# Two kinds of score matmuls in a bidirectional linear-attention block: in turn, or one kind after the other

## The chip, the cores and the metric

The kernel runs on one core of one Trainium2 chip. The metric is the device time of one execution in microseconds (us). The time before is the median of three executions; beside it stands one more execution, taken with the hardware profiler, from which all rows below come.

## What is computed

The program is two layers of an encoder trunk over 512 tokens of width 1024. A layer normalises its input, projects it, feeds three mixers (a state-space scan, a gated linear attention, a neighbourhood attention), mixes their outputs with gates and ends with a two-matrix MLP. The change touches the gated linear attention alone (GLA: 4 heads, key width 128, value width 256, chunks of 64 tokens, once forward and once backward). Cut to what matters, the reference computes for each head and direction:

```python
b = jnp.cumsum(g, axis=2)                       # log decay inside a chunk of 64
q_dec = q * jnp.exp(b)
att = jnp.einsum('bclhk,bcshk->bchls', q_dec, k * jnp.exp(-b))
att = jnp.where(tril, att, 0.0)                 # scores inside a chunk
o_intra = jnp.einsum('bchls,bcshv->bclhv', att, v)
states = jnp.einsum('bclhk,bclhv->bchkv', k * jnp.exp(b_last[:, :, None] - b), v)
...                                             # scan over the chunks
o_inter = jnp.einsum('bclhk,bchkv->bclhv', q_dec, s_prev)
```

## The kernel before, in words

All activations stay feature-major (128 features on the partitions, 512 tokens along the row). Most of the program is `feat` (L297) and `token` (L309): a weight of 128 x 1024 arrives by DMA, ScalarE rounds it to a high part (L285), VectorE subtracts to get the low part (L287), and TensorE multiplies in three products (L304 to L306, or L321 to L323) into a PSUM tile `pf` or `pt`. Three weights are under way at a time.

`gla_mix` (L649) is one head of the linear attention. Four pieces of 128 tokens (index `i`) hold two chunks of 64 each. For each direction `d` it builds on VectorE, ScalarE and GpSimd the decayed query `qd` (the tile `G_t`), two key tiles `ki` (`G_t` with 128 keys per piece, `G_kx` with 64) and the state keys `kw` (`G_w`). Then, at L694 to L702, it fills one PSUM tile `at` (a single buffer, `G_at`) per direction:

```python
T.matmul(at[:, i, b_], lhsT=ki[d][0][:, P * i: P * i + P], rhs=qs[0], start=True, stop=True)
T.matmul(at[a_, i, a_], lhsT=ki[d][1][:, i], rhs=qs[1], start=True, stop=True)
```

The first (L699) loads a weight of 128 columns and writes all 128 partitions; the second (L700) loads 64 columns and writes the 64 partitions `a_`. Both stream 64 query columns and contract over 128 rows. They are plain float32, and the hardware runs each as two passes, a weight load (LDWEIGHTS) and a matmul each: in the trace "x2" behind one of these lines is one such matmul. Two masked copies on VectorE (L701, L702) take `at` to the SBUF tiles `zt`, and GpSimd adds those to `G_A` (L704). After the scores, `kw` is transposed (L719) and copied (L721), the states are made (L731, L736, L738), and the output `po` is accumulated (L746, L748, L750). There are 2 layers x 4 heads x 2 directions = 16 of these blocks, each of four L699 and four L700.

The order of instructions on each engine is chosen at build time by a scheduler with a cost model: a block's matmuls are set between the `pf` or `pt` matmuls of the next projection, so that TensorE has other work while a head's VectorE work goes on. Each engine then runs its list strictly in that order.

Of the kernel before, what the change touches and what calls it, by code (L numbers as in the profile page):

```python
# [16 lines left out]
P = 128  # L17
# [182 lines left out]
def trunk(tc, a, out, layers=L, dbg=None):  # L200
    nc = tc.nc
    V, S, G, T = nc.vector, nc.scalar, nc.gpsimd, nc.tensor
    with ExitStack() as ctx:
# [178 lines left out]
        for l in range(layers):  # L382
# [263 lines left out]
            c4 = lambda ap, o: ap.rearrange("p (i o s) -> p i o s", i=4, o=2)[:, :, o]  # L646

            def gla_mix(h, q_, k_, v_, g_):
                qd, ki, kw, el, lg = [], [], [], [], []  # L649
# [44 lines left out]
                for d in range(2):  # L694
                    at = ph.p("at", (P, 4, P))
                    a_, b_ = slice(64 * d, 64 * d + 64), slice(64 - 64 * d, 128 - 64 * d)
                    for i in range(4):
                        qs = c4(qd[d], 1 - d)[:, i], c4(qd[d], d)[:, i]
                        T.matmul(at[:, i, b_], lhsT=ki[d][0][:, P * i: P * i + P], rhs=qs[0], start=True, stop=True)  # L699
                        T.matmul(at[a_, i, a_], lhsT=ki[d][1][:, i], rhs=qs[1], start=True, stop=True)  # L700
                    V.copy_predicated(zt[d][:, :, b_], trim[d][:, :, b_], at[:, :, b_])  # L701
                    V.copy_predicated(zt[d][a_, :, a_], trim[d][a_, :, a_], at[a_, :, a_])  # L702
                A = ph.t("A", (P, 4, P))
# [23 lines left out]
                for n in range(3):  # L727
                    pst_ = ph.p("at" if n == 2 else "x", (P, 2, 256))
                    for d in range(2):
                        i = n if d == 0 else 3 - n  # L730
                        T.matmul(pst_[:, d], lhsT=kt_[d][:, i], rhs=vv[i], start=True, stop=True)  # L731
                    for d in range(2):
                        i = n if d == 0 else 3 - n
# [56 lines left out]

            cur = gla_proj(0)
            y0 = gla_mix(0, *cur)
            for j in range(8):
                branch(0, j, nah, nal)
            gla_out(y0)
            cur = gla_proj(1)
            for h in range(1, 4):
                y = gla_mix(h, *cur)
                if h < 3:
                    cur = gla_proj(h + 1)  # L800
                    gla_out(y)
# [272 lines left out]
```

## Time and profile before

| | |
|---|---|
| median of 3 executions | 2468.46 us (2467.49 to 2468.6) |
| the profiled execution | 2469.9 us, span 2468.1 us |
| TensorE matmuls (PE) | busy 2452.2 us, 99% of the span, 12656 instructions |
| TensorE weight loads (PEld) | 2064.9 us, 84%, beside PE |
| VectorE (DVE) | 1425.8 us, 58% |
| ScalarE (ACT) | 1162.1 us, 47% |
| GpSimd (POOL) | 393.3 us, 16% |
| DMA engines, mean busy share | 31%, 101 GB/s |
| granted TensorE clock, mean | 0.998 of full speed |

PE's busy time counts a matmul from its start to a modelled end, so that it also covers time in which the array empties or waits for a weight. How long a piece of TensorE's work takes is therefore read from the distance between starts. On a timeline, a start is in us from the beginning of the span, and a group "x2" is two instructions in a row, its duration the time that they cover together.

### The profile page before, as it was taken

To read this page: it belongs to the slowest core of one execution; us is meant where nothing else is said; L and a number is where in the kernel's file an instruction comes from. 1 tells how busy PE (TensorE), PEld (TensorE's weight loads), DVE (VectorE), ACT (ScalarE), POOL (GpSimd) and SP (SyncE) were. 2 spreads that over 40 slices of the span, in tenths; PEclk is the share of its full clock that TensorE was granted. 3 is DMA by queue.
4 is the path that set the end of the run, shared out by engine and by line. 5 is a ranking of instruction groups with operands and counts; after the bars stand their busy time and mean duration, and the time that the engine had idled before them with its cause. 6 is when DMAs were issued, how large, how long until landed. Compare 5 with 4: busy or idle time off the path is not lost.

```text
span 2468.1 us, 32626 instructions
## 1 busy us (share of the span) xinstructions
PE 2452.2 (99%) x12656; PEld 2064.9 (84%) x12656; DVE 1425.8 (58%) x2148; ACT 1162.1 (47%) x2055; POOL 393.3 (16%) x333
## 2 busy tenths in 40 slices
PE   8999999999999999999999999999999999999999
PEld 7888889988788888888888888899878888888887
DVE  6776534587976554444447755345889665434443
ACT  4575435555855342332335654255568543422321
POOL 3132101112431110000122221011124312100000
PEclk9999999999999999999999999999999999999999
DMA  5221222223533322322332222222245333222232
GB/s 185 94 88 61 89 94 79 69 69 119 178 116 120 99 97 94 98 99 94 124 128 94 82 72 79 94 71 78 77 129 168 108 128 101 96 94 96 93 103 86
DMA packets 84603, 249.38 MB, mean 101 GB/s; under 512 B 9824, under 2 KB 15840, under 8 KB 84448
## 3 DMA queue, kind: packets, MB, share of 16 engines
q1 hardware_dynamic: 84016, 246.85, 30.5%
q8 instruction: 100, 1.64, 0.3%
q14 instruction: 55, 0.45, 0.1%
q10 hardware_dynamic: 432, 0.45, 0.1%
HBM read 242.80 MB, written 4.46 MB: 100 GB/s over the span
## 4 chain that ended last, share of the span: by engine, by line
PE 96%; DMA 2%; DVE 1%; ACT 1%; issue 0%; SPq 0%; DVEq 0%
PE pf L304 14%; PE pf L305 14%; PE pf L306 14%; PE F_pf L306 11%; PE F_pf L305 11%; PE F_pf L304 11%; PE pt L322 3%; PE pt L321 2%; PE pt L323 2%; PE N_po L569 2%; PE N_pt L562 1%; PE S_x L944 1%; PE G_at L699 1%; PE S_py L933 1%; PE G_at L700 1%; PE S_x L916 1%
## 5 line engine op out<-in xcount | busy, mean ns | idle before, releaser
L285 ACT ACTIVATE wh<-wr 128x1024 fp32r<-128x1024 f32 x378 | 400.2, 1059 | 938.7 <-PE F_pf L305 429.7
L287 DVE TENSOR_TENSOR wl<-wr,wh 128x1024 fp32r<-128x1024 f32 x378 | 485.7, 1285 | 188.4 <-ACT wh L285 186.6
L304 PE MATMUL pf<-xh,wh 128*128 128x512 f32 x1232 | 486.2, 395 | 7.6 <-DVE gl L592 3.7
L305 PE MATMUL pf<-xl,wh 128*128 128x512 f32 x1232 | 486.6, 395 | 0.7 <-DVE xl L349 0.7
L306 PE MATMUL pf<-xh,wl 128*128 128x512 f32 x1232 | 486.2, 395 | 0.0
L304 PEld LDWEIGHTS pf<-xh,wh 128*128 128x128 f32 x1232 | 232.2, 189 | 57.0 <-DVE gl L592 4.6
L306 PEld LDWEIGHTS pf<-xh,wl 128*128 128x128 f32 x1232 | 232.3, 189 | 49.5 <-issue 1.5
L305 PEld LDWEIGHTS pf<-xl,wh 128*128 128x128 f32 x1232 | 232.4, 189 | 48.9 <-issue 1.2
L304 PE MATMUL F_pf<-Ah,wh 128*128 128x512 f32 x640 | 248.4, 389 | 0.0
L306 PE MATMUL F_pf<-Ah,wl 128*128 128x512 f32 x640 | 247.8, 389 | 0.0
L305 PE MATMUL F_pf<-Al,wh 128*128 128x512 f32 x640 | 247.8, 389 | 0.0
L306 PE MATMUL F_pf<-xh,wl 128*128 128x512 f32 x512 | 200.1, 391 | 0.0
L305 PE MATMUL F_pf<-xl,wh 128*128 128x512 f32 x512 | 199.3, 389 | 0.0
L304 PE MATMUL F_pf<-xh,wh 128*128 128x512 f32 x512 | 199.3, 389 | 0.0
L1051 DVE TENSOR_TENSOR F_x<-F_x,F_pf 128x512 f32<-128x512 f32 x64 | 44.0, 688 | 205.6 <-PE F_pf L306 205.6
L322 PE MATMUL pt<-wl,xh 128*128 128x256 f32 x512 | 146.1, 286 | 0.0
L323 PE MATMUL pt<-wh,xl 128*128 128x256 f32 x512 | 145.9, 286 | 0.0
L321 PE MATMUL pt<-wh,xh 128*128 128x256 f32 x512 | 144.9, 284 | 0.0
L304 PEld LDWEIGHTS F_pf<-Ah,wh 128*128 128x128 f32 x640 | 120.2, 188 | 25.0
L305 PEld LDWEIGHTS F_pf<-Al,wh 128*128 128x128 f32 x640 | 120.1, 188 | 25.0
L306 PEld LDWEIGHTS F_pf<-Ah,wl 128*128 128x128 f32 x640 | 120.1, 188 | 24.8
L1044 DVE SCALAR_TENSOR_TENSOR F_v<-F_pf,rx 128x512 f32<-128x512 f32 x64 | 44.1, 691 | 159.5 <-PE F_pf L306 159.5
(313 smaller groups left out, 4257.1 us busy)
## 6 DMA issues: line engine op xcount, KB each, us to landing
wr<-pk SPq DMA_DIRECT2D x378, 512.0 KB, 3.3
N_bias<-bias SPq DMA_DIRECT2D x48, 256.0 KB, 2.9
S_E<-acd SPq DMA_DIRECT2D x32, 256.0 KB, 4.3
S_eB<-acd SPq DMA_DIRECT2D x32, 256.0 KB, 3.8
S_eb<-ead SPq DMA_DIRECT2D x64, 96.0 KB, 3.5
F_x<-xt SPq DMA_DIRECT2D x15, 256.0 KB, 5.2
xd<-F_x SPq DMA_DIRECT2D x8, 256.0 KB, 2.0
F_x<-xd SPq DMA_DIRECT2D x8, 256.0 KB, 4.8
```

The source lines that it names most:

```text
L285: S.activation(hi, raw, AF.Copy)
L287: V.tensor_tensor(lo, raw, f(hi), ALU.subtract)
L304: T.matmul(ps, lhsT=hi[:, c], rhs=rh[k], start=k == 0, stop=False)
L305: T.matmul(ps, lhsT=hi[:, c], rhs=rl[k], start=False, stop=False)
L306: T.matmul(ps, lhsT=lo[:, c], rhs=rh[k], start=False, stop=k == KT - 1)
L321: T.matmul(o, lhsT=rh[k][:, s], rhs=hi[:, c], start=k == 0, stop=False)
L322: T.matmul(o, lhsT=rh[k][:, s], rhs=lo[:, c], start=False, stop=False)
L323: T.matmul(o, lhsT=rl[k][:, s], rhs=hi[:, c], start=False, stop=k == KT - 1)
L562: T.transpose(pt[:, i, kb], s[:, i, P * kb: P * (kb + 1)], ident)
L569: T.matmul(po[r, P * cb: P * (cb + 1)], lhsT=vv[:, v0 + kb, r], rhs=ptS[:, i, kb], start=kb == 0, stop=kb == 1)
L1044: V.scalar_tensor_tensor(v_, ps, 0.0, rbc, ALU.max, ALU.mult)
L1051: V.tensor_tensor(xT[j], xT[j], ps, ALU.add)
```

## The change

Per direction, the loop over the four pieces is split in two: first the four matmuls with 128 keys, then the four with 64 keys. Operands, results and the number of instructions stay as they are.

```diff
                     at = ph.p("at", (P, 4, P))
                     a_, b_ = slice(64 * d, 64 * d + 64), slice(64 - 64 * d, 128 - 64 * d)
                     for i in range(4):
-                        qs = c4(qd[d], 1 - d)[:, i], c4(qd[d], d)[:, i]
-                        T.matmul(at[:, i, b_], lhsT=ki[d][0][:, P * i: P * i + P], rhs=qs[0], start=True, stop=True)
-                        T.matmul(at[a_, i, a_], lhsT=ki[d][1][:, i], rhs=qs[1], start=True, stop=True)
+                        T.matmul(at[:, i, b_], lhsT=ki[d][0][:, P * i: P * i + P], rhs=c4(qd[d], 1 - d)[:, i],
+                                 start=True, stop=True)
+                    for i in range(4):
+                        T.matmul(at[a_, i, a_], lhsT=ki[d][1][:, i], rhs=c4(qd[d], d)[:, i], start=True, stop=True)
                     V.copy_predicated(zt[d][:, :, b_], trim[d][:, :, b_], at[:, :, b_])
                     V.copy_predicated(zt[d][a_, :, a_], trim[d][a_, :, a_], at[a_, :, a_])
```

In the changed kernel these lines are L698 and L701, and every later line is one further down (L719 is L720 there, L731 is L732). On TensorE, the first block of the program (head 0, forward; `G_x` the transposed keys, `pf` the projection that goes on) ended before with these rows, the last two of its four turns:

```order
L699 MATMUL G_at_2817<-G_t_25_2770,G_t_26_2771 128x64
L700 MATMUL G_at_2817<-G_t_25_2770,G_kx_2798 64x64
L699 MATMUL G_at_2817<-G_t_25_2770,G_t_26_2771 128x64
L700 MATMUL G_at_2817<-G_t_25_2770,G_kx_2798 64x64
L719 MATMUL G_x_2845<-con,G_w_2793 128x128 x4
L305 MATMUL pf_2992<-xl_175,wh_2921 128x512
```

And the same place in the changed kernel, with the whole block and the projection matmul ahead of it:

```order
L304 MATMUL pf_2992<-xh_174,wh_2921 128x512
L698 MATMUL G_at_2817<-G_t_25_2770,G_t_26_2771 128x64 x4
L701 MATMUL G_at_2817<-G_t_25_2770,G_kx_2798 64x64 x4
L720 MATMUL G_x_2845<-con,G_w_2793 128x128 x4
L305 MATMUL pf_2992<-xl_175,wh_2921 128x512
```

The eight matmuls stand in two runs of four instead of eight runs of one, in this block and in the 15 others (96 rows fewer on TensorE, six a block); what stands before and after them here is the same.

Around the backward blocks of heads 1 and 2 the scheduler also moved a few neighbours by one or two projection matmuls. On TensorE, head 1, backward, where the states (`G_x`, `G_at` at L731, now L732) are made ("-" the kernel before, "+" the changed one):

```order
+L732 MATMUL G_at_3885<-G_gvg_3586,G_kwT_3858 128x256
+L732 MATMUL G_x_3871<-G_gvg_3586,G_kwT_3869 128x256
+L732 MATMUL G_x_3878<-G_gvg_3583,G_kwT_3858 128x256
+L732 MATMUL G_x_3878<-G_gvg_3586,G_kwT_3869 128x256
+L732 MATMUL G_at_3885<-G_gvg_3583,G_kwT_3869 128x256
 L323 MATMUL pt_4055<-wh_3935,xl_179 128x256
-L731 MATMUL G_at_3885<-G_gvg_3586,G_kwT_3858 128x256
-L731 MATMUL G_x_3871<-G_gvg_3586,G_kwT_3869 128x256
-L731 MATMUL G_x_3878<-G_gvg_3583,G_kwT_3858 128x256
-L731 MATMUL G_x_3878<-G_gvg_3586,G_kwT_3869 128x256
-L731 MATMUL G_at_3885<-G_gvg_3583,G_kwT_3869 128x256
```

The state matmuls stand ahead of one projection matmul that they stood behind; the other moves are of the same kind. VectorE's list has a few swaps in heads 1 and 2: L710 (L711 after), which overwrites the query `qd` that the block reads, now stands ahead of L682 in head 1 and ahead of L677 in head 2. The lists of ScalarE, GpSimd and the DMA queue are the same but for line numbers.

## Rows read from the trace of the kernel before

**Rows 1.** Page, part 1: busy time of the engines; part 4: chain by engine.

```profile
PE 2452.2 (99%) x12656; PEld 2064.9 (84%) x12656; DVE 1425.8 (58%) x2148; ACT 1162.1 (47%) x2055; POOL 393.3 (16%) x333
...
PE 96%; DMA 2%; DVE 1%; ACT 1%; issue 0%; SPq 0%; DVEq 0%
```

**Rows 2.** Windows: busy us per engine, then granted clock, DMA share, GB/s.

```profile
280.00:560.00 280.00, 280.00 (x1583) 244.66 (x1582) 155.73 (x255) 133.05 (x202) 29.66 (x22) 1.00 0.23 78
1506.00:1786.00 280.00, 280.00 (x1582) 244.74 (x1582) 156.12 (x255) 133.40 (x202) 29.66 (x22) 1.00 0.24 78
500.00:560.00 60.00, 60.00 (x282) 49.72 (x281) 51.85 (x84) 34.27 (x52) 8.07 (x5) 1.00 0.21 71
```

**Rows 3.** Tile G_at: line, engine, count, min/median/max ns, first and last start.

```profile
L699 PE MATMUL G_at<-G_t,G_t x128: 217/275/324, 284.0 to 1756.7; 128*128 128x64 f32 x128
L700 PE MATMUL G_at<-G_t,G_kx x128: 221/246/271, 284.3 to 1757.0; 128*64 128x64 f32 x128
```

**Rows 4.** Timeline of PE, first block: start, duration, line, shape, passes.

```profile
284.00 0.33 PE L699 MATMUL G_at<-G_t,G_t 128*128 128x64 f32 x2
284.26 0.33 PE L700 MATMUL G_at<-G_t,G_kx 128*64 128x64 f32 x2
284.52 0.43 PE L699 MATMUL G_at<-G_t,G_t 128*128 128x64 f32 x2
284.88 0.33 PE L700 MATMUL G_at<-G_t,G_kx 128*64 128x64 f32 x2
...
286.39 0.66 PE L719 MATMUL G_x<-con,G_w 128*128 128x128 f32 x4
```

**Rows 5.** Timeline of PEld (weight loads), same block; then one load each by tile.

```profile
284.52 0.30 PEld L699 LDWEIGHTS G_at<-G_t,G_t 128*128 128x128 f32 x2
284.88 0.19 PEld L700 LDWEIGHTS G_at<-G_t,G_kx 128*64 128x64 f32 x2
...
L699 PEld LDWEIGHTS G_at<-G_t,G_t x128: 185/188/192, 283.8 to 1756.7; 128*128 128x128 f32 x128
L700 PEld LDWEIGHTS G_at<-G_t,G_kx x128: 132/134/137, 284.3 to 1757.0; 128*64 128x64 f32 x128
```

**Rows 6.** Timeline, PE: runs of one shape elsewhere (2, 128 and 128 columns streamed).

```profile
75.04 0.95 PE L501 MATMUL N_v<-bsr,sq 128*128 128x2 f32 x8
...
607.92 1.50 PE L916 MATMUL S_x<-S_xw,S_bt 128*128 128x128 f32 x12
...
123.47 0.60 PE L569 MATMUL N_po<-N_pT,N_vb 128*64 128x128 f32 x4
```

**Rows 7.** Timeline, PEld: one short run; chain: a matmul of 256 columns, two passes.

```profile
567.49 0.32 PEld L813 LDWEIGHTS S_x<-con,gtmp 32*128 32x128 f32 x4 [0.35 <-issue]
...
306.20 0.43 PE G_po L748 x2
```

**Rows 8.** Timelines of DVE and PE: blocks and states, what they wait for or release.

```profile
289.85 0.43 DVE L702 COPY_PREDICATED zt<-con,G_at 64x256 f32<-64x256 int32 x1
291.90 0.33 PE L699 MATMUL G_at<-G_t,G_t 128*128 128x64 f32 x2
...
413.37 0.33 PE L700 MATMUL G_at<-G_t,G_kx 128*64 128x64 f32 x2
413.75 0.69 DVE L682 TENSOR_TENSOR G_t<-G_t,G_q 128x512 f32<-128x512 f32 x1
...
542.38 0.86 DVE L738 SCALAR_TENSOR_TENSOR G_st<-G_st,de,G_at 128x256 f32<-128x256 f32 x2
544.62 0.59 PE L748 MATMUL G_po<-G_st,G_t 128*128 128x256 f32 x2
```

**Rows 9.** Timeline of PE at a wait in the state-space part; windows behind it.

```profile
622.11 0.49 PE L304 MATMUL pf<-xh,wh 128*128 128x512 f32 x1 [2.08 <-DVE gl L592]
...
620.00:624.00 4.00, 1.92 (x8) 1.31 (x7) 3.96 (x11) 4.00 (x12) 0.00 (x0) 0.93 0.70 252
624.00:628.00 4.00, 4.00 (x28) 3.38 (x28) 3.96 (x8) 4.00 (x13) 1.07 (x1) 0.64 0.52 162
```

## The prediction

> **What bounds the kernel.** I read the page first. PE is busy 2452.2 us of a span of 2468.1 us, and the chain of work that ended last lies on PE for 96% of the span [rows 1]. So TensorE's own list sets the time, and a piece of it that gets shorter shortens the run, as long as nothing that it then reaches sooner is late. Second, the windows over the linear-attention stretch of either layer: PE is covered for 280.00 of 280.00 us in both, at a granted clock of 1.00 (the 2.4 GHz level), while VectorE is covered for 155.73 and ScalarE for 133.05 [rows 2]. In these stretches lie all 16 blocks of the change [rows 3], by their first and last start, so there is no wait in them that could swallow what a block saves.
>
> Third, the timeline of one block, for the time between starts. An L699 that follows an L700 begins at 284.52, the next L700 at 284.88: a turn of 0.36 us. An L700 begins at 284.26 and the next L699 at 284.52: a turn of 0.26 us [rows 4]. The whole block, from the first L699 at 284.00 to the first transpose at 286.39, takes 2.39 us. That is the first L699, whose first weight was loaded beside the projection matmul ahead of it (284.00 to 284.26, 0.26 us), three turns of 0.36 and four of 0.26, together 2.38 us.
>
> Fourth, what a turn is made of. Two weight loads of L699 cover 0.30 us and one is recorded with 0.188, so the second starts 0.11 us after the first; for L700 it is 0.19 less 0.134, or 0.06 us [rows 5]. Two loads would be 0.22 and 0.12 us. The turns are longer by 0.36 - 0.22 = 0.14 and by 0.26 - 0.12 = 0.14 us. The same 0.14 us stands behind either kind, each time where a weight of 128 columns and one of 64 follow each other: the next load does not start until the matmul before it has left the array. Where the shape stays the same, no such gap is to be seen. Eight passes of L501 (128 columns, two streamed) cover 0.95 us, twelve of L916 cover 1.50 us; with a record of 0.25 to 0.28 us for the last one, that is 0.10 and 0.11 us a pass [rows 3, 6]. Four passes of L569, which loads 64 columns and streams 128, cover 0.60 us, or 0.11 a pass. So runs of one shape go at the rate of their loads or of their matmuls, with no gap of 0.14 between them.
>
> **The change, part by part.**
>
> *The order inside a block.* Before, the shape changes at each of the eight turns' ends: eight switches. After, it changes twice, behind the last L699 and behind the last L700. Six switches go, per block 6 x 0.14 = 0.84 us. Written out: the L699 run takes 0.26 for the first and 3 x 0.22 for the rest, which is 0.92 us with the switch at its end; the L700 run takes 3 x 0.12 + 0.26 = 0.62 us; together 1.54 instead of 2.38 us. Over 16 blocks that is 16 x 0.84 = 13.4 us.
>
> *The unknown in it* is how fast a long run of 64-column loads with 64 streamed columns goes, since no row shows one longer than two passes. Bounds: the load's own distance inside a pair is 0.06 us, and a run of four passes at L813 covers 0.32 us with 0.13 to 0.14 for the last load, 0.06 a pass [rows 7]. The far end is L569 with 0.11 a pass [rows 6], but there twice as many columns stream. I take 0.06, since the streamed width is that of L700. At 0.11 an L700 turn in the run would be 0.22 and save only 0.04; a block would save 3 x 0.14 + 3 x 0.04 = 0.54 us, and the sum would be 8.6 us. At the other end the gap is 0.15 us where the roundings of 0.01 fall the other way, and the sum is 16 x 6 x 0.15 = 14.4 us.
>
> *What is reached sooner.* Each thing that PE reaches behind a block now comes up to 0.84 us earlier. The backward scores need `at` free again: L702 ends at 290.28 and the next block starts at 291.90, 1.62 us of room. The closest that I found is L748 behind L738, 543.24 to 544.62, 1.38 us, and L738 itself waits for PE's states, so it moves along [rows 8]. Both are larger than 0.84 us, so I cost them at nothing; the cover is TensorE's projection work, and if it were gone a wait would take back at most what a block saves.
>
> *The moved neighbours.* State matmuls that pass a projection matmul of 256 columns come some 0.1 us sooner, which the room above also covers. Their shape is the projection's, so no switch is added. The masked copy L701 may start sooner, because L699's results are complete earlier; no one waits for it, so nothing is gained. On VectorE, L710 may not run before the block has read `qd`, and it now stands ahead of L682 in head 1, in the slot at 413.75, with L682 and the next block's keys queued behind it. The last L700 began at 413.37 and covered 0.33 us [rows 8], so it was done at 413.70, and will be done 0.84 us sooner: no wait. DMA issues and the other engines' lists stand as before.
>
> *The sum.* 13.4 us off the profiled 2469.9 us gives 2456.5 us. That execution lies 1.4 us above the median of the others; the same 13.4 us off the median of 2468.46 us gives 2455.0 us, 0.54% less.
>
> **Rivals.**
>
> *Loads do not run ahead in a run.* If a load had to wait for the matmul ahead of it whenever both use the same rows, a pass would be load plus matmul. A matmul of 256 columns takes 0.43 / 2 = 0.215 us [rows 7], one of 64 then 0.05; passes become 0.16 and 0.11, turns 0.32 and 0.22, each 0.04 less than now. A block saves 3 x 0.04 + 3 x 0.04 = 0.24 us and the time is 2468.46 - 3.8 = 2464.6 us. Against it: L916 has a load of 0.11 and 128 streamed columns, also 0.11, and a pass takes 0.11, not 0.22 [rows 6]. In the Trainium skill, the page "TensorE: Matmul & The Clock Gate", part 3, section "The mechanism", says that a weight load overlaps with matmuls in flight only when their row groups differ. Both kinds here contract over all 128 rows, so by that rule the gain would be this small one. The trace of L916 disagrees with it: its loads and matmuls use the same 128 rows and overlap. Chance 0.05.
>
> *The gain is partly taken by waits.* The last two blocks of a layer lie in a stretch where VectorE is covered for 51.85 of 60 us [rows 2]. If VectorE could not move forward there, and the state-space part behind it then waited, up to 2 x 2 x 0.84 = 3.4 us would be lost, and with the 0.11 us pass the gain would fall to 5.2 us: 2463.3 us. Chance 0.05.
>
> *Slower: a new wait that drops the clock.* Where PE waited 2.08 us for VectorE at 622.11, the clock granted shortly after was 0.93 and 0.64 of full speed in two windows of 4 us [rows 9]: a part of the time at the 1.2 GHz level, worth 4 x 0.07 + 4 x 0.36 = 1.7 us. If every head's L748 came to wait as long, 8 x (2.1 + 1.7) = 30.4 us would be lost against 13.4 gained: 2485.5 us. It decides once L738 is late by more than its 1.38 us of room in all heads; nothing in the change delays it. Chance 0.02.
>
> *The change does not do what it says.* A scheduler could set the kinds in turn again; the rows of the order above show two runs of four, so this has no chance of its own.
>
> **How the numbers follow.** The forecast, a gain of 8.6 to 14.4 us, has a chance of 0.88. The clock's fall at 622 may or may not come in another run, which moves the time by 1.7 us either way. So the time lies between 2468.46 - 14.4 - 1.7 = 2452.4 and 2468.46 - 8.6 = 2459.8 us; I give 2452.0 to 2460.0. About 0.2% (4.9 us) is what a measurement of this kernel can tell from no change. The forecast and the partly taken gain lie beyond it (0.93), the rival with loads held back lies within (0.05), the new wait is slower (0.02).
>
> **What would show it.** In the changed profile, a block from its first L698 to the first L720 should take 1.5 to 1.6 us; eight passes of L698 should start 0.11 us apart and eight of L701 0.06; one gap of some 0.14 us should be left between the kinds and one at the end. PE should still cover the whole linear-attention stretch, now some 7 us shorter per layer. The forecast is wrong if blocks take over 1.9 us, or if they take 1.5 us and PE shows waits behind L732, L747 or L749 that were not there.

## The result, and the profile after

The changed kernel takes 2454.40 us (median of 6 executions, 2453.42 to 2455.18) against 2467.67 us of the kernel before (6 executions, 2465.82 to 2468.6). The ratio is 0.9946, with a 95% interval of 0.9934 to 0.9957: 13.3 us less. The forecast was 2455.0 us, from 13.4 us less.

The first lines of the page of the changed kernel, to be held against [rows 1]: PE is busy 13.3 us less, the other engines within 3 us of what they were.

```profile
span 2452.7 us, 32628 instructions
PE 2438.9 (99%) x12656; PEld 2057.8 (84%) x12656; DVE 1423.0 (58%) x2148; ACT 1161.7 (47%) x2055; POOL 394.8 (16%) x333
```

The timeline of PE over the first block (start, duration, line, shape, passes), which answers to [rows 4], and under it that of the weight loads, which answers to [rows 5]:

```profile
283.57 1.00 PE L698 MATMUL G_at<-G_t,G_t 128*128 128x64 f32 x8
284.50 0.68 PE L701 MATMUL G_at<-G_t,G_kx 128*64 128x64 f32 x8
285.11 0.66 PE L720 MATMUL G_x<-con,G_w 128*128 128x128 f32 x4
285.52 0.48 PE L305 MATMUL pf<-xl,wh 128*128 128x512 f32 x1
```

```profile
283.34 1.09 PEld L698 LDWEIGHTS G_at<-G_t,G_t 128*128 128x128 f32 x8
284.50 0.54 PEld L701 LDWEIGHTS G_at<-G_t,G_kx 128*64 128x64 f32 x8
```

From the first score matmul to the first transpose the block takes 285.11 - 283.57 = 1.54 us, where it took 2.39 us; the two runs take 0.93 and 0.61 us. All 16 blocks agree within 0.01 us. Eight loads of 64 columns cover 0.54 us, and with 0.138 us for the last [the tile's rows below] that is 0.058 us a load.

The tile's rows (count, then min/median/max ns, first and last start), against [rows 3] and [rows 5]:

```profile
L698 PE MATMUL G_at<-G_t,G_t x128: 217/275/275, 283.6 to 1739.9; 128*128 128x64 f32 x128
L701 PEld LDWEIGHTS G_at<-G_t,G_kx x128: 132/138/138, 284.5 to 1740.5; 128*64 128x64 f32 x128
```

The longest record of a 128-key matmul falls from 324 to 275 ns: it was the one that began behind a change of shape.

Windows over the linear-attention stretches, against [rows 2] (length of the window, busy us of PE, PEld, DVE, ACT, POOL, then clock, DMA share, GB/s):

```profile
280.00:552.00 272.00, 272.00 (x1578) 240.14 (x1577) 153.65 (x252) 132.49 (x201) 29.64 (x22) 1.00 0.24 79
1498.00:1770.00 272.00, 272.00 (x1579) 240.13 (x1578) 153.64 (x251) 131.61 (x200) 29.65 (x22) 1.00 0.24 79
```

PE is still covered from end to end; no wait took the place of the gaps. To see where the time went I cut the span at three marks in each layer: the first gate projection of the linear attention (`G_ga`), the first transpose of the state-space part (`S_x<-con,gtmp`) and the first matmul of the output projection (`F_pf`). Between the first two, both layers went from 298.56 to 291.74 us, 6.82 us less each, which is 8 blocks x 0.85 us. Between the last two, the state-space part and what follows it went from 280.35 to 277.91 us in the first layer and from 277.64 to 278.73 us in the second. The rest of a layer did not move (647.46 us from the first layer's output projection to the second layer's gate projection in both kernels).

The two profiled executions differ by 15.4 us of span, 2 us more than the medians. The piece above what the blocks gave, 1.8 us, lies in the state-space parts (1.4 us in sum) and at the start (0.4 us). That one of these parts shrank and the other grew is in part the clock: the fall that stood at 624 us before [rows 9] is gone, though the wait ahead of it is still there (2.1 us, at 613 us now), and another stands in the second layer, behind the same kind of wait (1.86 us, up to 1830.40). Windows of the changed kernel, the first over the wait at 613 us and what follows it:

```profile
612.00:628.00 16.00, 14.47 (x87) 11.71 (x89) 15.93 (x32) 13.84 (x41) 6.94 (x5) 1.00 0.61 202
1826.00:1830.00 4.00, 2.54 (x12) 1.75 (x11) 4.00 (x11) 3.29 (x9) 0.82 (x2) 1.00 0.72 222
1830.00:1834.00 4.00, 3.60 (x11) 2.46 (x13) 3.93 (x8) 4.00 (x12) 0.00 (x0) 0.58 0.37 95
```

### The profile page after: what moved, and what is told of

Read it like the earlier page. It is cut to its first block, busy times and chain, and to the rows that moved or that the text cites. A ratio compares the mean times of both kernels' runs of the same rounds, so it can differ in the third digit from the quotient of the medians.

```text
span 2452.7 us, 32628 instructions
## 1 busy us (share of the span) xinstructions
PE 2438.9 (99%) x12656; PEld 2057.8 (84%) x12656; DVE 1423.0 (58%) x2148; ACT 1161.7 (47%) x2055; POOL 394.8 (16%) x333
## 4 chain that ended last, share of the span: by engine, by line
PE 97%; DMA 1%; DVE 1%; ACT 1%; issue 0%; SPq 0%; DVEq 0%
PE pf L304 15%; PE pf L305 15%; PE pf L306 14%; PE F_pf L306 11%; PE F_pf L305 11%; PE F_pf L304 11%; PE pt L322 3%; PE pt L323 3%; PE pt L321 3%; PE N_po L569 2%; PE N_pt L562 1%; PE S_x L945 1%; PE S_py L934 1%; PE S_x L917 1%; PE N_sc L546 1%; PE N_sc L547 1%
```

## The experiments

The theory is that each change between weights of 128 and of 64 columns costs TensorE some 0.14 us, as if it waited until the matmuls in flight have left the array, and that the block's time follows the number of such changes. The rivals: only a full separation helps; turning between tiles or between regions of the PSUM tile is what costs; the moved neighbours brought the gain. Diffs are against the changed kernel.

### Four changes of shape instead of two

```diff
-                    for i in range(4):
-                        T.matmul(at[:, i, b_], ...
-                    for i in range(4):
-                        T.matmul(at[a_, i, a_], ...
+                    for i0 in (0, 2):
+                        for i in (i0, i0 + 1):
+                            T.matmul(at[:, i, b_], ...
+                        for i in (i0, i0 + 1):
+                            T.matmul(at[a_, i, a_], ...
```

> Two L699, two L700, twice over, so four changes of shape per block instead of eight (before) or two (after). Theory, each change of shape between 128-column and 64-column weights costs about 0.14 us: a block takes 0.26 + 0.22 + 0.12 + 0.26 + 0.36 + 0.22 + 0.12 + 0.26 = 1.82 us from its first matmul to the first transpose, 0.56 us less than before, in all 16 x 0.56 = 9.0 us less than before (about 2459 us). Rival, only a complete separation of the two kinds helps (each return to the other kind costs what the eight turns cost): a block stays near 2.4 us and the time near 2468 us. Rival, the gain of the change came from the moved neighbours and not from the block: the time does not follow the number of changes of shape.

Measured: 2459.05 us (ratio to before 0.9964, 0.9951 to 0.9977), 9.1 us less than the 2468.18 us of the kernel before on the same chip. Its timeline:

```profile
283.10 0.55 PE L699 MATMUL G_at<-G_t,G_t 128*128 128x64 f32 x4
283.58 0.45 PE L702 MATMUL G_at<-G_t,G_kx 128*64 128x64 f32 x4
283.96 0.66 PE L699 MATMUL G_at<-G_t,G_t 128*128 128x64 f32 x4
284.55 0.45 PE L702 MATMUL G_at<-G_t,G_kx 128*64 128x64 f32 x4
284.92 0.66 PE L721 MATMUL G_x<-con,G_w 128*128 128x128 f32 x4
```

The block takes 1.82 us. With eight, four and two changes it takes 2.39, 1.82 and 1.54 us: 0.57 / 4 and 0.28 / 2, both 0.14 us for a change. Both rivals fall: each return to the other kind costs its own 0.14 us and no more, and the blocks alone account for the time (16 x 0.57 = 9.1 us), so the moved neighbours are not the source.

### No change of shape, but still in turn

The 64-key matmul takes 128 columns from a key tile that is one piece longer (its first or last piece zero), and writes 128 partitions; only the 64 that were wanted are read. The two kinds stand in turn again.

```diff
-                    kx = ph.t("kx", (P, 4, 64))
-                    V.tensor_tensor(kx, c4(t2, d), c4(k_, d), ALU.mult)
+                    kx = ph.t("kx", (P, 5, 64))
+                    G.memset(kx[:, 4 - 4 * d], 0.0)
+                    V.tensor_tensor(kx[:, d: d + 4], c4(t2, d), c4(k_, d), ALU.mult)
...
+                        T.matmul(at[:, i, a_], lhsT=flat(ki[d][1][:, i: i + 2]), rhs=c4(qd[d], d)[:, i], ...
```

> The two kinds in turn as before, but the 64-key matmuls load 128 columns (the keys beside them or zeros in the other half, whose results are written and never read): eight turns, no change of shape at all. Adds one small GpSimd memset per block. Theory (the change of shape empties the array, not the change of operand or of destination): loads follow each other at 0.11 us, 16 passes take 15 x 0.11 = 1.65 us from the first matmul to the next load, 0.7 us less than before and 0.1 us more than after; time about 2468 - 16 x 0.7 = 2456 to 2458 us. Rival (turning between two tiles or two regions of the PSUM bank is what costs): a block stays at 2.4 us and the time near 2468 us.

Measured: 2460.56 us (0.9969, 0.9958 to 0.998). The first rows of its block and the transpose behind it:

```profile
283.43 0.33 PE L699 MATMUL G_at<-G_t,G_t 128*128 128x64 f32 x2
283.59 0.39 PE L701 MATMUL G_at<-G_t,G_kx 128*128 128x64 f32 x2
283.82 0.39 PE L699 MATMUL G_at<-G_t,G_t 128*128 128x64 f32 x2
...
285.16 0.60 PE L721 MATMUL G_x<-con,G_w 128*128 128x128 f32 x4
```

The turns are still there, and the gaps are not: behind the first one a matmul begins every 0.22 us, the two loads and nothing else, and 1.73 us lie between the first score matmul and the first transpose (the latter's load starts at 1.62). So it is the shape, not the turn between tiles or PSUM regions. The time, however, is 2.6 to 4.6 us above the 2456 to 2458 us that were expected from such blocks. That is taken up below.

### The short kind first

```diff
-                    for i in range(4):
-                        T.matmul(at[:, i, b_], ...
                     for i in range(4):
                         T.matmul(at[a_, i, a_], ...
+                    for i in range(4):
+                        T.matmul(at[:, i, b_], ...
```

> The run of four with 64 keys first, then the run of four with 128 keys: again two changes of shape, at the start of the block and in its middle, none at its end. Theory (the number of changes decides): the work from the last projection matmul to the first transpose takes as long as in the changed kernel within 0.1 us, and the time is within 2 us of the changed kernel's 2454.4 us. Rival (it matters that the long weights come first, because their first load hides behind the projection): the block is longer by the 0.1 us or more of a load that no longer hides, 16 x 0.1 = 1.6 us or more.

Measured: 2459.79 us (0.9965, 0.9952 to 0.9978), 5 us above the changed kernel: more than the theory allows, and more than the first load of the rival explains, as the rows show. The first block and the projection matmuls on either side:

```profile
281.73 0.39 PE L305 MATMUL pf<-xl,wh 128*128 128x512 f32 x1
282.05 0.68 PE L698 MATMUL G_at<-G_t,G_kx 128*64 128x64 f32 x8
282.66 1.10 PE L700 MATMUL G_at<-G_t,G_t 128*128 128x64 f32 x8
283.60 0.60 PE L720 MATMUL G_x<-con,G_w 128*128 128x128 f32 x4
283.96 0.48 PE L306 MATMUL pf<-xh,wl 128*128 128x512 f32 x1
```

From the projection matmul to the transpose are 1.87 us here, and 285.11 - 283.34 = 1.77 us in the changed kernel (its last projection matmul begins at 283.34). But the transpose's own load starts 0.11 us before it here and with it there, so most of this is made good: the next projection matmul begins 2.23 us after the one ahead of the block here (283.96 - 281.73) and 2.18 us there (285.52 - 283.34). The order of the two kinds costs 0.05 us a block, 0.8 us in all. The linear-attention stretch takes 291.08 us, 0.66 us less than that of the changed kernel, but it holds five projection matmuls fewer (0.23 us each, 1.1 us), which stand in the state-space part here; without that it would be 0.5 us longer. The rest of the loss is in the state-space part, 282.61 and 281.37 us. There TensorE waits for VectorE at places where the changed kernel does not:

```profile
PE S_x L945 <- DVE S_st L924: 3.7, 6, 1.6
PE S_py L934 <- DVE S_E L906: 2.9, 3, 2.0
```

(waiter, producer, us in total, times, longest). The changed kernel has a wait there that this one has not, of the projection for the VectorE operation at L592, which reads an earlier `pf`:

```profile
PE pf L304 <- DVE gl L592: 4.0, 2, 2.1
```

With 0.4 us more for another, that is 4.4 us against 6.6 us: the waits that show make up only 2.2 us of the loss. The lists show where the difference begins. The scheduler sets TensorE's order in the state-space part in one of three ways in these kernels, and which one depends on small shifts before it. The kernels of before, after, with pairs and with split loads (below) have one list there; this kernel and the one with wide loads share another, in which TensorE reaches the state matmuls L945 before VectorE has their states ready. (The kernel with loads of 32 columns, at the end, has a third.)

### Is it the list or the block?

Two kernels turn the order round in one head alone (4 of 16 blocks): in the last head, which gives the second list, and in the first head, which leaves the first.

```diff
-                    for i in range(4):
-                        T.matmul(at[:, i, b_], ...
-                    for i in range(4):
-                        T.matmul(at[a_, i, a_], ...
+                    for kind in ((1, 0) if h == 3 else (0, 1)):
+                        for i in range(4):
+                            if kind:
+                                T.matmul(at[a_, i, a_], ...
+                            else:
+                                T.matmul(at[:, i, b_], ...
```

(the second with `h == 0`.)

> The changed kernel, with the 64-key run first in the last head alone (4 of 16 blocks). Its list on TensorE for the state-space part is then the one that the kernel with the 64-key run first everywhere and the one with wide 64-key loads have; the list of before and of the changed kernel is another. Theory (that second list costs the state-space part 3 to 4 us per layer, whatever the blocks look like): its state-space part takes 281 to 283 us per layer instead of 277 to 280, and the time is 2459 to 2462 us. Rival (the blocks with the 64-key run first cost the 5 us themselves): a quarter of 5 us, so 2455.5 to 2456 us.

> The changed kernel, with the 64-key run first in the first head alone (4 of 16 blocks). Its list on TensorE for the state-space part is that of the changed kernel. Theory: the time is the changed kernel's, 2453 to 2456 us. Rival (the blocks themselves cost): as much as with the last head turned round, so no difference between the two kernels.

Measured: 2459.07 us with the last head turned round (2458.24 to 2461.53), 2454.91 us with the first (2453.96 to 2455.33). The same edit to the same number of blocks costs 4.2 us more in one place than in the other, and with a quarter of the blocks the loss is nearly the whole one: it goes with the list. In the first layer the state-space part runs from 558.9 to 840.8 us in the one and from 560.3 to 839.8 us in the other (first start of each row; a row each of the two kernels):

```profile
L817 PE MATMUL S_x<-con,gtmp x8: 220/222/244, 558.9 to 1779.3; 32*128 32x32 f32 x8
L304 PE MATMUL F_pf<-Ah,wh x640: 389/389/390, 840.8 to 2451.4; 128*128 128x512 f32 x160
```

```profile
L817 PE MATMUL S_x<-con,gtmp x8: 220/222/244, 560.3 to 1779.3; 32*128 32x32 f32 x8
L304 PE MATMUL F_pf<-Ah,wh x640: 389/389/389, 839.8 to 2448.6; 128*128 128x512 f32 x160
```

That is 281.9 and 279.5 us; in the second layer it is 280.5 us, just under the 281 us that were expected, and 277.5 us. The waits of the first of the two are again those for the states, which the other does not show; it shows the wait of the changed kernel instead (a row each):

```profile
PE S_x L948 <- DVE S_st L927: 3.6, 6, 1.3
```

```profile
PE pf L304 <- DVE gl L592: 3.8, 2, 2.1
```

How the 5.2 us between them are made up can be read in part from windows over these parts (both layers of the one, then both of the other):

```profile
558.90:840.80 281.90, 278.18 (x1415) 228.00 (x1415) 203.07 (x309) 165.01 (x340) 79.17 (x65) 1.00 0.40 129
1779.10:2059.50 280.40, 277.99 (x1414) 227.90 (x1414) 202.98 (x309) 164.75 (x340) 78.70 (x65) 1.00 0.40 130
```

```profile
560.30:839.80 279.50, 276.81 (x1409) 228.03 (x1409) 205.46 (x309) 163.32 (x338) 77.60 (x65) 0.99 0.41 130
1779.10:2056.70 277.60, 275.41 (x1410) 226.99 (x1410) 206.43 (x309) 162.51 (x338) 77.24 (x65) 1.00 0.41 131
```

PE is not covered for 6.1 us in the one and for 4.9 us in the other, so idle time is some 1.3 us of the difference. Five projection matmuls more in each layer are 2.3 us, which the linear-attention stretch is spared. Two more changes of width in each layer are an estimated 0.6 us at 0.14 us. The last 1 us was not traced to a place, and the fall of the clock in the first layer of the second kernel (0.99) hides some more.

Over all kernels of this study, the six profiles with the first list besides that of before show 277.4 to 279.6 us for this part (before: 280.4 and 277.6), the four with the second list 280.5 to 282.6. The longest of either are those in which the clock fell within the part; where it did not fall, the first list takes 277.4 to 278.2 us and the second 280.5 to 282.3 us. Of that distance 1.1 us are the five projection matmuls that the second list does behind the mark instead of before it.

### Precedence for the states

The two VectorE operations that carry the states on were given precedence in the scheduler, to take the waits of the second list away, and in two kernels without these waits for comparison.

```diff
-                    V.tensor_tensor(he(tm), he(prev), ...
-                    V.tensor_tensor(cur, cur, tm, ALU.add)
+                    with hp():
+                        V.tensor_tensor(he(tm), he(prev), ...
+                    with hp():
+                        V.tensor_tensor(cur, cur, tm, ALU.add)
```

> The kernel with the 64-key run first, whose blocks were as short as the changed kernel's but whose time was 5 us longer, with one more edit: in the state-space part the two VectorE operations that carry the states on (the ones TensorE was seen waiting for) are given precedence in the scheduler's list. Theory (the 5 us were lost to VectorE's order in the state-space part, which the scheduler set otherwise, and not in the blocks): the waits of L945 for the states go, 2 to 5 us less than 2459.8 us. Rival (the 5 us belong to the block order): the time stays at 2459 to 2460 us though these waits go.

> The changed kernel with the same precedence for the states. Its trace shows no wait for the states either: within 2 us of 2454.4 us by the theory. If the time rises by 3 us or more, the state-space part is as sensitive to VectorE's order as the loss of the 64-first kernel says, in the other direction.

Measured: 2459.23 us with the short kind first, and 2454.19 us for the changed kernel with the same edit. The first of these says nothing about the theory that it was made for: TensorE's list stayed the second one, and the waits stayed too (4.1 us for the states, eight times). The other is the changed kernel's time, as expected. Which move in the second list makes the states late stays open, and so does whether the loss would go with the waits.

### One shape in the whole block

Each 128-key matmul becomes two of 64 columns, one to each half of the partitions.

```diff
                     for i in range(4):
-                        T.matmul(at[:, i, b_], lhsT=ki[d][0][:, P * i: P * i + P], ...
+                        for r in (slice(0, 64), slice(64, 128)):
+                            T.matmul(at[r, i, b_], lhsT=ki[d][0][:, P * i + r.start: P * i + r.stop], ...
```

> Each 128-key matmul split into two of 64 columns, one to the lower and one to the upper 64 partitions, then the four 64-key matmuls: one shape in the whole block, 24 passes of 64 columns, changes of shape only at its two ends. Theory, if neighbouring passes to different halves do not overlap: 24 x 0.058 = 1.39 us plus one gap at either end, about 1.65 us counted from the same point, 0.1 us more than after: 2456 us. If passes to different halves run side by side, as the pairs of L933 starting 5 ns apart in the trace suggest: 16 x 0.058 = 0.93 plus the gaps, about 1.2 us, 0.33 us less than after, 16 x 0.33 = 5 us less: 2449 us. Rival (more instructions make it slower): 8 more matmuls per block at the 0.11 us of a pass, 1.54 + 0.9 = 2.4 us, 2468 us.

Measured: 2450.50 us (0.9928, 0.9913 to 0.9943), 3.9 us less than the changed kernel's median. Its block on PE, and its loads:

```profile
283.36 0.39 PE L304 MATMUL pf<-xh,wh 128*128 128x512 f32 x1
283.68 0.69 PE L699 MATMUL G_at<-G_t,G_t 128*64 128x64 f32 x16
284.19 0.63 PE L702 MATMUL G_at<-G_t,G_kx 128*64 128x64 f32 x8
284.75 0.66 PE L721 MATMUL G_x<-con,G_w 128*128 128x128 f32 x4
```

```profile
283.68 0.55 PEld L699 LDWEIGHTS G_at<-G_t,G_t 128*64 128x64 f32 x16 [0.35 <-issue]
284.14 0.55 PEld L702 LDWEIGHTS G_at<-G_t,G_kx 128*64 128x64 f32 x8
```

Sixteen loads that go to the two halves by turns cover the same 0.55 us as eight that go to one half: the halves work side by side. From the last projection matmul to the transpose the block takes 1.39 us instead of 1.77 us, 0.38 us less, in all 6 us; the time fell by 3.9 us. The linear-attention stretch is 290.15 us, 1.6 us less per layer where 8 x 0.38 = 3.0 would be. In three blocks of each layer the scheduler set two or five projection matmuls between the first score matmul and the rest, which brings two more changes of shape into each of them (22 in the layer instead of 16) and takes the first pair out of its run. By the starts of their rows these blocks are some 0.45 us longer for it, 1.4 us a layer, which is what is missing.

With the precedence for the states added:

> The split kernel (all 64-column weights in the block) with the same precedence for the states. Its trace shows no wait for the states, so by the theory that only waits that are there can be won back the time stays within 2 us of 2450.5 us; the other order of VectorE may cost or give a microsecond or two. Rival (the precedence itself helps): 3 us or more less.

Measured: 2449.71 us (2449.28 to 2450.89), the same within what a run can tell. These two are the fastest kernels of the study.

### Loads of 32 columns

```diff
-                        T.matmul(at[a_, i, a_], lhsT=ki[d][1][:, i], ...
+                        for r in (0, 32):
+                            T.matmul(at[64 * d + r: 64 * d + r + 32, i, a_], lhsT=ki[d][1][:, i, r: r + 32], ...
```

(and the two kinds in turn again.)

> In turn again, but each 64-key matmul is split into two of 32 columns, so that the shapes alternate between 128 and 32 columns. In the trace of before, matmuls with 32-column weights at L454 and L854, written to the lowest partitions, follow and precede 128-column ones with no gap (0.23 us behind a projection matmul, 0.11 us to the next transpose). Theory A, only 64-column weights empty the array: no gap in the block, 8 passes at 0.11 and 16 at 0.03 to 0.06 us, about 1.4 to 1.9 us. Theory B, any weight narrower than the array does, and the rows of L454 and L854 are special because they are written to the lowest partitions (first 32): eight gaps of 0.14 us or more remain, 2.4 us or more, perhaps fewer in the forward blocks, whose first 32 columns go there, than in the backward ones.

Measured: 2464.8 us in a single run, 4.0 us less than before on the same chip, where the blocks give 16 x 0.09 = 1.4 us; its list in the state-space part is the third one (277.7 and 278.1 us), and one run does not say more. Its block:

```profile
283.13 0.33 PE L698 MATMUL G_at<-G_t,G_t 128*128 128x64 f32 x2
283.39 0.31 PE L701 MATMUL G_at<-G_t,G_kx 128*32 128x64 f32 x4
283.62 0.43 PE L698 MATMUL G_at<-G_t,G_t 128*128 128x64 f32 x2
283.99 0.30 PE L701 MATMUL G_at<-G_t,G_kx 128*32 128x64 f32 x4
...
285.43 0.66 PE L721 MATMUL G_x<-con,G_w 128*128 128x128 f32 x4
```

The gaps are there, and the block takes 2.30 us: a change to 32 columns costs a gap as one to 64 does, in the forward blocks, which begin at the lowest partitions, as in the backward ones. Theory A falls. Theory B holds in the main, but its reason for the exception does not, since a first load at the lowest partitions has its gap too.

## Why the prediction was right

*TensorE's list sets the time, and the stretch has no wait.* Right: the stretch is shorter by what the blocks are shorter by, to 0.02 us, and PE is covered throughout.

*Six changes of shape at 0.14 us.* Right: 0.85 us per block against 0.84, and the runs with four and with no changes of shape show the same price from two other sides. The two runs were put at 0.92 and 0.62 us and take 0.93 and 0.61.

*The unknown, the pace of a long run of short loads.* 0.06 us was taken, between 0.06 and 0.11; it is 0.058. The distance inside a pair of L700 loads was the row to take. The run at L813 that was set beside it was not its like: it loads 128 columns of 32 rows, for transposes, and streams 32 [rows 7], so that its 0.06 us is the same by luck. That a run of 64-column loads keeps the pace of a pair was a bet, and it came true.

*What is reached sooner, and the moved neighbours.* No new wait in the stretch, as the room of 1.4 us and more against 0.84 said.

*Loads that do not run ahead.* This rival would have left 2464.6 us. It falls with L701: a load of 64 columns alone covers some 0.06 us, and eight of them with their eight matmuls between run at that pace. The rule of the Trainium skill's page "TensorE: Matmul & The Clock Gate", part 3, section "The mechanism", that was set against it does not describe these runs. What does is a sentence in the Trainium skill's page "TensorEngine Tiling (Array Packing)", section "Key Properties": changing the tiling mode drains the engine, changing only the tile does not. The traces of the score blocks agree on both halves, with 0.14 us for a change of shape, and with sixteen loads to alternating halves in 0.55 us. What the engine does in these 0.14 us no run here shows; the weights at the end of this document show no such gap.

*Waits that take part of the gain, and the wait that drops the clock.* No new wait came in the changed kernel; the clock fell in the second layer (0.58 above), behind a wait that the kernel before had too (1.7 us there, without a fall). That the place was named rightly shows in the kernels with the second list: there TensorE waits for VectorE in the state-space part and some 4 to 5 us of the gain go, of which the waits that show are the smaller part. What was not seen is the cause: not a VectorE that can't move forward, but a list that the scheduler sets anew. The changed kernel kept the list of before; this could have been read from the two lists, and the prediction did not say it: it had no term for a new list, and that it needed none was luck as far as its own words go.

## What to carry to other kernels

Where narrow and full-width matmuls stand by turns on TensorE, count the changes of weight width and price them at the distance between starts, here 0.14 us each: put matmuls of one width together, or make all of one width, and where both halves of the columns are to be filled let narrow ones to the two halves alternate. When a scheduler sets the order, compare its lists for the whole program and not only around the edit: an edit that saves the same time in its own place lost 4 us of it in another part, through a list that only one of two such edits changed.

## What the runs showed that I had not expected

Alternating 64-column loads to the two halves of the partitions go twice as fast as a run to one half: 16 in 0.55 us against 8 in 0.55 us.

The narrow weights at L854 of the kernel before show no gap on either side: the projection matmul ahead starts at 599.10, the four passes at 599.33, and the 128-column transposes 0.43 us after that.

```profile
599.10 0.39 PE L306 MATMUL pf<-Ah,wl 128*128 128x512 f32 x1
599.33 0.60 PE L854 MATMUL S_x<-con,S_sm 128*32 128x128 f32 x4
599.76 0.49 PE L864 MATMUL S_x<-con,X_bc 128*128 128x128 f32 x3
```

They too load 32 columns. In the score block the same width has gaps. These four are transposes, of one pass each, stream 128 columns and write a PSUM tile of 32 partitions; which of this sets them apart, if any of it does, was not tested.
